# One transposed copy moved from ScalarE to VectorE, with other stage priorities, in a hybrid decoder layer

## The chip, the cores and the metric

One core of a Trainium2 chip runs the kernel. The metric is device microseconds of one execution. The kernel before takes 232.57 us, the median of 3 runs (232.31 to 232.76). Engines are named as the profile names them: PE is TensorE (PEld its weight loads), DVE is VectorE, ACT is ScalarE, POOL is GpSimd, SP is SyncE, which issues most DMAs.

## What is computed

One decoder layer on x (1 x 256 x 1024, float32). One projection of x is cut into four groups of 6 heads of 64 channels each; each group's output is gated, all four are concatenated, projected back to 1024 columns, and added to x under a layer norm:

```python
p = x @ w_in                                   # 1024 -> 5906 columns, four groups
y_a = moba_attention(...)  * silu(a_g)         # causal softmax attention, ALiBi
y_b = rms_norm(ssd_mixer(...) * silu(s_z))     # Mamba-2 scan, chunks of 128
y_c = dilated_attention(...) * silu(c_g)       # softmax over three dilations
y_d = rms_norm(gated_delta_chunked(...)) * silu(d_g)
out = layer_norm(alpha * x + concat(y_a, y_b, y_c, y_d) @ w_out)
```

The part that the change touches belongs to the gated delta rule. In chunks of 64 tokens it needs the inverse of a unit lower triangular matrix for each head:

```python
Lm = where(strict, (k * beta) @ k.T * decay, 0)
T = triangular_solve(eye + Lm, eye, lower=True, unit_diagonal=True)
u = T @ (v * beta)
w = T @ (k * beta * exp(g_cum))
```

## The kernel before

The float32 projections run as three matmul passes over high and low parts in float32r: `split` (line 447) takes a block of weights that `load` (432) brought by DMA into `raw`, copies it to `whi` on ScalarE, and VectorE subtracts to get `wlo`; TensorE then multiplies hi by hi, lo by hi, hi by lo. Rings of four `raw`, four `whi` and four `wlo` buffers keep this stream in program order. Around the stream stand the stages of the four groups: convolutions ("conv ..."), gates, decays, "norm k", "products" (which makes the matrices `M` and `A`), "blocks", "join", "delta", "state" and "scan", "scores", "values" and "attention" for the two softmax groups a and c, then "out" and the layer norms.

"blocks" starts at line 806. It inverts the 48 diagonal blocks of 32 x 32 (12 head-chunks of 128 tokens, 4 blocks each). Four DMAs move the blocks of `M` to DRAM (`dM`), one brings them back with one block on each of 48 partitions (`BL`, line 817). Then 31 elimination steps of two VectorE instructions each (a product into `tmp`, a subtraction into `Ub`) build the inverse, 62 instructions in sequence. `Tb`, the transposed copy of `Ub` inside each partition, is made at line 825; `Tb` goes to DRAM as `dT`, `Ub` as `dU`, and both come back as `T` (a part of the tile `TZ`) and `U`, spread over the 128 partitions. "join" combines pairs of 32-blocks to blocks of 64 with small matmuls, and "delta" (848) runs the recurrence. Memory is shared by tags: `BL` lies where the decay matrix `E` of the delta group was (tag s4), and `biasa`, the biases of attention a (977), come into the same place later.

The order on every engine isn't the program's. `Plan.run` (221) simulates a list schedule with costs written in the code and gives each engine its order; the order on an engine is then fixed, SP's DMAs included. Each operation has a rank: its `way` to the end, in us of the planner's costs, plus a bias, which is the stage's entry in `PRIO` and a correction for single steps in `STEPS`. `AHEAD` lets an engine wait a little for an operation of better rank, `LIMIT` says how many of the eight PSUM banks a kind of tile may hold at once, `STICK` favours matmuls of the mode that TensorE is in. The lines that decide:

```python
rank = [-int(o["way"] * 1000 + 0.5) - math.floor(o["bias"] * 1000 + 0.5) for o in ops]
...
t = min(at.values()) + AHEAD.get(e, 0.0)
k = min((max(at[i], t), rank[i] - stay(ops[i]), i) for i in at)
```

Every instruction is recorded through the planner, so nearly all have line 381 in the profile; tiles tell them apart.

Of the kernel before, what the change touches and what calls it, by code (L numbers as in the profile page):

```python
# [12 lines left out]
AF = mybir.ActivationFunctionType  # L13
# [37 lines left out]
def _biases():  # L51
# [12 lines left out]
NSM = 478  # L64
WARM = 8
STREAM = 1.0
SWITCH, PORT, AHEAD = 0.17, 0.9, {"dve": 0.033, "pe": 0.172, "pool": 0.066}
CUTS = (((0, 512), (512, 512)), ((0, 512), (512, 256), (768, 256)))
SHARE = [[slice(a, b) for a, b in v] for v in (
    ((0, 256), (256, 512)), ((512, 1024),), ((0, 512), (512, 1024)), ((0, 384), (384, 768), (768, 1024)))]  # L70
HELD = 5
HOLD = {10: (("hold_hi", "cvg", 1), ("hold_lo", "s3", 1))}
PRIO = {"split": -6.8, "conv k": 146.3, "gate d": -1265.8, "conv q": 1492.8, "gate s": 701.0, "steps": 1693.7,
        "decay d": 1542.9, "norm k": 4481.3, "products": 382.5, "norm q": 5697.9, "decay s": -3554.0,
        "values c": 663.3, "conv v": 174.6, "blocks": 42.6, "join": -2709.8, "delta": 4073.4, "conv bc": 149.8,
        "conv x": -58.8, "state": -630.8, "scan": 3483.0, "scores c": -913.9, "attention c": 9085.5,
        "scores a": 5133.5, "values a": -8452.1, "attention a": 1239.3, "out": -958.7, "out 0": -3694.0,
        "out 1": -5902.3, "ln 0": -1382.8, "ln 1": -1514.8}
CONST = -5, -4, -3
NRAW = 4  # L80
POOL = (6,)
POOLS = {"ps": (8, 512, F), "work": (3, W, F), "workd": (2, W, F), "workx": (1, W, F), "workg": (2, W, F), "cy": (3, S, F), "p": (3, W, F), "mx": (3, 4, F), "pt": (3, W, F), "oss": (2, 6, F), "sss": (2, 1, F), "srs": (2, 1, F)}
RINGS = {"raw": 4, "whi": 4, "wlo": 4}
STEPS = {"conv q 0": {"pe": -2.7}, "gate s 4": {"dve": -198.5}, "products 2": {"dve": 421.0},
# [9 lines left out]
         "attention a 5": {"dve": 0.6, "act": 142.2}, "attention a 6": {"act": -596.3},  # L94
         "attention a 10": {"act": -288.8}, "out 4": {"pe": 22.2}}
LIMIT = {"pj": 6, "g": 3, "ed": 6, "es": 6, "n": 4, "m": 5, "d": 2, "o": 4, "td": 2, "b": 1, "s": 2, "ts": 5, "c": 3, "ct": 6, "cv": 4, "a": 6, "at": 1, "av": 1}
BEGIN, SLOW = 1.2, 2.5
BESIDE = {(64, 128): 0.85, (128, 64): 0.62}
STICK = 1.0


class Plan:
# [289 lines left out]
def hybrid_layer(ctx, tc, plan, xT, x, w_in, w_out, convw, small, ln_g, ln_b, cst, biases, out):  # L392
    nc = tc.nc
    pe, act, dve, pool, sp = (plan.engine(n, e) for n, e in (
        ("pe", nc.tensor), ("act", nc.scalar), ("dve", nc.vector), ("pool", nc.gpsimd), ("sp", nc.sync)))
    pj = plan.engine("pe", nc.tensor, True)
# [94 lines left out]
    b = bank("pj")  # L491
# [244 lines left out]
    b = bank("ed")  # L736
# [7 lines left out]
    for i in range(2):  # L744
        b = bank("n")
# [12 lines left out]
        b = bank("n")  # L758
# [19 lines left out]
    for i in range(2):  # L778
        b, sq = bank("n"), work()
# [17 lines left out]
    for i in range(2):  # L797
        b = bank("n")
# [14 lines left out]
    BL, Ub, Tb = (t[:, :1024].rearrange("p (a b) -> p a b", a=32) for t in (BL, UbT, Tb))  # L813
# [6 lines left out]
    for j in range(31, 0, -1):  # L820
        n = 32 - j
        tv = tmp[:, :j * n].rearrange("p (a b) -> p a b", a=j)
        dve.tensor_mul(tv, BL[:, 0:j, j:j + 1].to_broadcast([48, j, n]), Ub[:, j:j + 1, j:32].to_broadcast([48, j, n]))
        dve.tensor_sub(Ub[:, 0:j, j:32], Ub[:, 0:j, j:32], tv)
    act.activation(Tb, Ub.rearrange("p a b -> p b a"), AF.Copy)
    sp.dma_start(dT, Tb)
    sp.dma_start(dU, Ub)
    for k in range(0, 4, 2):
# [274 lines left out]
```

## Time and profile before

| | us |
|---|---|
| median of 3 runs | 232.57 (232.31 to 232.76) |
| profiled execution | 233.04 |
| its span, first to last instruction | 231.3 |
| busy PE, DVE, ACT, POOL | 218.9, 174.5, 140.0, 24.2 |
| mean granted TensorE clock | 0.994 |

The span is shorter than the execution's own time by what lies around it. Busy shares are means over stages with different limits, so they have to be read by stretch; idle time counts only on the engine that holds up the end, and there the question is what ended it.

### The profile page before, as it was taken

To read this page: it belongs to the slowest core of one execution; us is meant where nothing else is said; L and a number is where in the kernel's file an instruction comes from. 1 tells how busy PE (TensorE), PEld (TensorE's weight loads), DVE (VectorE), ACT (ScalarE), POOL (GpSimd) and SP (SyncE) were. 2 spreads that over 40 slices of the span, in tenths; PEclk is the share of its full clock that TensorE was granted. 3 is DMA by queue.
4 is the path that set the end of the run, shared out by engine and by line. 5 is a ranking of instruction groups with operands and counts; after the bars stand their busy time and mean duration, and the time that the engine had idled before them with its cause. 6 is when DMAs were issued, how large, how long until landed. Compare 5 with 4: busy or idle time off the path is not lost. (4 is left out here: it accounts for less than half of the span.)

```text
span 231.3 us, 4530 instructions
## 1 busy us (share of the span) xinstructions
PE 218.9 (95%) x1679; PEld 202.6 (88%) x1679; DVE 174.5 (75%) x414; ACT 140.0 (61%) x297; POOL 24.2 (10%) x28
## 2 busy tenths in 40 slices
PE   8999999999999999999989999798999999999970
PEld 3999899998989999999979998687889998888870
DVE  2764999998599989998999984351677996635274
ACT  4765965738953666754469936999932854442210
POOL 7005021200110000000000000000221300000071
PEclk9999999999999999999999999999999999999997
DMA  5999766893934975489550249940523052663013
GB/s 170 312 335 361 209 195 201 211 241 81 273 102 102 234 187 155 128 225 277 150 163 29 68 101 320 270 110 9 180 67 119 1 184 91 211 242 94 0 68 113
DMA packets 46101, 38.10 MB, mean 165 GB/s; under 512 B 5616, under 2 KB 42608, under 8 KB 46080
## 3 DMA queue, kind: packets, MB, share of 16 engines
q1 hardware_dynamic: 45648, 37.43, 55.2%
q10 hardware_dynamic: 432, 0.39, 0.5%
q8 instruction: 13, 0.21, 0.4%
q14 instruction: 8, 0.07, 0.1%
HBM read 36.18 MB, written 1.64 MB: 163 GB/s over the span
## 5 line engine op out<-in xcount | busy, mean ns | idle before, releaser
L381 ACT ACTIVATE whi<-raw 128x1024 fp32r<-128x1024 f32 (+3 forms) x57 | 56.9, 1004 | 40.9 <-PE ps L381 31.1
L381 DVE TENSOR_TENSOR wlo<-raw,whi 128x1024 fp32r<-128x1024 f32 (+3 forms) x56 | 64.2, 1154 | 21.3 <-ACT whi L381 17.5
L381 PE MATMUL ps<-xhi,whi 128*128 128x256 f32 x272 | 41.9, 289 | 0.2
L381 PE MATMUL ps<-xlo,whi 128*128 128x256 f32 x272 | 41.8, 286 | 0.0
L381 PE MATMUL ps<-xhi,wlo 128*128 128x256 f32 x272 | 39.8, 284 | 0.0
L381 PEld LDWEIGHTS ps<-xhi,whi 128*128 128x128 f32 x272 | 36.0, 190 | 2.6 <-ACT whi L381 1.5
L381 PEld LDWEIGHTS ps<-xlo,whi 128*128 128x128 f32 x272 | 36.4, 191 | 0.8 <-issue 0.3
L381 PEld LDWEIGHTS ps<-xhi,wlo 128*128 128x128 f32 x272 | 35.7, 189 | 0.0
L381 PE MATMUL ps<-whi,mix 128*128 128x512 f32 (+1 forms) x110 | 28.7, 350 | 0.0
L381 ACT ACTIVATE p<-p,mx 128x256 f32<-128x256 f32 (+1 forms) x48 | 19.5, 444 | 3.6 <-DVE mx L381 3.6
L381 PEld LDWEIGHTS ps<-whi,mix 128*128 128x128 f32 x110 | 19.1, 188 | 2.7
L381 DVE SCALAR_TENSOR_TENSOR cy<-ps,cw,cy 128x253 f32<-128x253 f32 (+2 forms) x48 | 20.8, 473 | 0.8 <-ACT cy L381 0.7
L381 PE MATMUL ps<-wlo,mix 128*128 128x512 f32 (+1 forms) x55 | 19.3, 350 | 0.0
L381 PE MATMUL ps<-whi,xlo 128*128 128x384 f32 (+2 forms) x64 | 17.3, 344 | 0.0
L381 PE MATMUL ps<-whi,xhi 128*128 128x384 f32 (+2 forms) x64 | 16.9, 345 | 0.0
L381 PE MATMUL ps<-wlo,xhi 128*128 128x384 f32 (+2 forms) x64 | 16.4, 340 | 0.0
L381 POOL TENSOR_SCALAR_AFFINE_SELECT Es<-Es 128x1536 f32<-128x1536 f32 x1 | 1.5, 1548 | 100.7 <-ACT Es L381 100.7
L381 PEld LDWEIGHTS ps<-whi,xlo 128*128 128x128 f32 x64 | 11.6, 188 | 0.1
L381 PEld LDWEIGHTS ps<-wlo,xhi 128*128 128x128 f32 x64 | 11.6, 188 | 0.1
L381 PEld LDWEIGHTS ps<-whi,xhi 128*128 128x128 f32 x64 | 11.2, 188 | 0.5 <-ACT whi L381 0.2
L381 PEld LDWEIGHTS ps<-wlo,mix 128*128 128x128 f32 x55 | 10.4, 188 | 1.4
L381 DVE TENSOR_TENSOR Ub<-Ub 48x31 f32<-48x31 f32 (+15 forms) x31 | 10.3, 332 | 0.7
(219 smaller groups left out, 309.4 us busy)
## 6 DMA issues: line engine op xcount, KB each, us to landing
raw<-in_w_in_dram SPq DMA_DIRECT2D x30, 512.0 KB, 4.4
raw<-in_w_out_dram SPq DMA_DIRECT2D x12, 512.0 KB, 3.4
raw<-in_w_in_dram SPq DMA_DIRECT2D x8, 384.0 KB, 3.3
lead<-in_w_in_dram SPq DMA_DIRECT2D x7, 256.0 KB, 5.0
raw<-in_w_in_dram SPq DMA_DIRECT2D x4, 396.0 KB, 6.6
raw<-in_w_in_dram SPq DMA_DIRECT2D x4, 390.0 KB, 4.7
x<-in_x_dram SPq DMA_DIRECT2D x2, 512.0 KB, 5.1
xr<-in_xT_dram SPq DMA_DIRECT2D x7, 128.0 KB, 5.0
```

Of the source, the lines that this page charges most:

```text
L381: self.plan.add(eng, lambda: f(*a, **k), cost, outs, ins, dma, mode, port or (eng == "pool" and not dma), place, slow)
```

## The change

The copy of `Ub`, transposed inside each partition, into `Tb` is made by VectorE's `tensor_copy` instead of ScalarE's activation with the function Copy. The two DMAs behind it and everything else that is computed stay. The tables that the planner ranks by have other values: `PRIO` for each stage, `STEPS` for single steps, `LIMIT` for 12 of its kinds, `AHEAD` (no entry for GpSimd any more, VectorE's 0.038 in place of 0.033) and `STICK` (5.0 in place of 1.0). With them the order on every engine can differ.

```diff
@@ -64,39 +64,39 @@
 NSM = 478
 WARM = 8
 STREAM = 1.0
-SWITCH, PORT, AHEAD = 0.17, 0.9, {"dve": 0.033, "pe": 0.172, "pool": 0.066}
+SWITCH, PORT, AHEAD = 0.17, 0.9, {"dve": 0.038, "pe": 0.172}
 CUTS = (((0, 512), (512, 512)), ((0, 512), (512, 256), (768, 256)))
 SHARE = [[slice(a, b) for a, b in v] for v in (
     ((0, 256), (256, 512)), ((512, 1024),), ((0, 512), (512, 1024)), ((0, 384), (384, 768), (768, 1024)))]
 HELD = 5
 HOLD = {10: (("hold_hi", "cvg", 1), ("hold_lo", "s3", 1))}
-PRIO = {"split": -6.8, "conv k": 146.3, "gate d": -1265.8, "conv q": 1492.8, "gate s": 701.0, "steps": 1693.7,
-        "decay d": 1542.9, "norm k": 4481.3, "products": 382.5, "norm q": 5697.9, "decay s": -3554.0,
-        "values c": 663.3, "conv v": 174.6, "blocks": 42.6, "join": -2709.8, "delta": 4073.4, "conv bc": 149.8,
-        "conv x": -58.8, "state": -630.8, "scan": 3483.0, "scores c": -913.9, "attention c": 9085.5,
-        "scores a": 5133.5, "values a": -8452.1, "attention a": 1239.3, "out": -958.7, "out 0": -3694.0,
-        "out 1": -5902.3, "ln 0": -1382.8, "ln 1": -1514.8}
+PRIO = {"split": -6.8, "conv k": 261.5, "gate d": -1103.0, "conv q": 2491.5, "gate s": 854.7, "steps": 959.8,
+        "decay d": 1365.0, "norm k": 3635.6, "products": 309.8, "norm q": 6289.3, "decay s": -3915.3,
+        "values c": 756.8, "conv v": 164.5, "blocks": 659.4, "join": -2148.0, "delta": 5895.1, "conv bc": 151.7,
+        "conv x": -1545.1, "state": -1603.0, "scan": 1806.4, "scores c": -1852.9, "attention c": 8700.6,
+        "scores a": 5582.8, "values a": -6773.5, "attention a": 279.6, "out": -172.9, "out 0": -2742.4,
+        "out 1": -6301.6, "ln 0": -357.4, "ln 1": -2147.1}
 CONST = -5, -4, -3
 NRAW = 4
 POOL = (6,)
 POOLS = {"ps": (8, 512, F), "work": (3, W, F), "workd": (2, W, F), "workx": (1, W, F), "workg": (2, W, F), "cy": (3, S, F), "p": (3, W, F), "mx": (3, 4, F), "pt": (3, W, F), "oss": (2, 6, F), "sss": (2, 1, F), "srs": (2, 1, F)}
 RINGS = {"raw": 4, "whi": 4, "wlo": 4}
-STEPS = {"conv q 0": {"pe": -2.7}, "gate s 4": {"dve": -198.5}, "products 2": {"dve": 421.0},
-         "values c 1": {"pe": -170.4}, "values c 3": {"pe": -72.9}, "conv v 1": {"pe": 468.1},
-         "delta 6": {"pe": -9.9}, "conv bc 1": {"dve": -32.7}, "conv bc 2": {"dve": 93.5, "pe": -2.3},
-         "conv x 0": {"dve": 91.0}, "conv x 2": {"dve": -38.6},
-         "scores c q 2": {"dve": 44.6, "pe": 161.4}, "scores c k 1": {"pe": 58.2},
-         "scores c k 2": {"pe": 29.3}, "attention c 2": {"act": -39.3},
-         "attention c 5": {"act": -123.9}, "attention c 6": {"dve": 134.5, "pe": 56.8},
-         "attention c 9": {"pe": 44.5}, "attention c 10": {"dve": 4.9, "pe": 22.8},
-         "scores a k 2": {"pe": 64.6}, "values a 1": {"pe": 460.5}, "attention a 0": {"pe": -0.2},
-         "attention a 1": {"act": 12.1}, "attention a 2": {"act": 1.5}, "attention a 4": {"pe": -0.1},
-         "attention a 5": {"dve": 0.6, "act": 142.2}, "attention a 6": {"act": -596.3},
-         "attention a 10": {"act": -288.8}, "out 4": {"pe": 22.2}}
-LIMIT = {"pj": 6, "g": 3, "ed": 6, "es": 6, "n": 4, "m": 5, "d": 2, "o": 4, "td": 2, "b": 1, "s": 2, "ts": 5, "c": 3, "ct": 6, "cv": 4, "a": 6, "at": 1, "av": 1}
+STEPS = {"conv q 0": {"pe": -36.8}, "gate s 4": {"dve": -212.7}, "products 2": {"dve": 290.2},
+         "products 4": {"dve": -58.6}, "values c 0": {"pe": 26.5}, "values c 1": {"pe": -203.2},
+         "values c 2": {"pe": 26.6}, "conv v 0": {"pe": 332.1}, "conv v 1": {"dve": -76.4},
+         "delta 2": {"pe": 4.2}, "conv bc 0": {"act": 102.4, "dve": 75.4}, "conv bc 2": {"pe": -3.4},
+         "conv x 0": {"pe": 1.9}, "conv x 1": {"dve": -117.8, "pe": 5.6}, "conv x 2": {"dve": -16.3},
+         "state": {"pe": 107.2}, "scores c k 0": {"pe": -422.2}, "attention c 1": {"act": 32.7},
+         "attention c 2": {"dve": -44.4}, "attention c 5": {"pe": -2.2},
+         "attention c 6": {"act": 179.6}, "attention c 7": {"pe": -93.8},
+         "attention c 9": {"dve": -47.1, "act": 156.4}, "attention c 10": {"act": 82.1},
+         "values a 1": {"pe": 127.3}, "attention a 0": {"pe": -0.2}, "attention a 1": {"act": 70.0},
+         "attention a 2": {"act": 12.6}, "attention a 5": {"act": 414.1},
+         "attention a 6": {"act": -44.5}, "attention a 10": {"act": -4.1}, "out 4": {"pe": 62.0}}
+LIMIT = {"pj": 6, "g": 2, "ed": 6, "es": 3, "n": 6, "m": 4, "d": 5, "o": 3, "td": 3, "b": 1, "s": 4, "ts": 3, "c": 6, "ct": 4, "cv": 5, "a": 6, "at": 1, "av": 1}
 BEGIN, SLOW = 1.2, 2.5
 BESIDE = {(64, 128): 0.85, (128, 64): 0.62}
-STICK = 1.0
+STICK = 5.0
 
 
 class Plan:
@@ -822,7 +822,7 @@
         tv = tmp[:, :j * n].rearrange("p (a b) -> p a b", a=j)
         dve.tensor_mul(tv, BL[:, 0:j, j:j + 1].to_broadcast([48, j, n]), Ub[:, j:j + 1, j:32].to_broadcast([48, j, n]))
         dve.tensor_sub(Ub[:, 0:j, j:32], Ub[:, 0:j, j:32], tv)
-    act.activation(Tb, Ub.rearrange("p a b -> p b a"), AF.Copy)
+    dve.tensor_copy(Tb, Ub.rearrange("p a b -> p b a"))
     sp.dma_start(dT, Tb)
     sp.dma_start(dU, Ub)
     for k in range(0, 4, 2):
```

## Rows read from the trace of the kernel before

**Rows 1.** The page, part 1: busy us, share of the span, instructions
```profile
PE 218.9 (95%) x1679; PEld 202.6 (88%) x1679; DVE 174.5 (75%) x414; ACT 140.0 (61%) x297; POOL 24.2 (10%) x28
```

**Rows 2.** Chain that ended last: start us, us, what (its longest piece)
```profile
167.37 56.85 PE ps L381 x378
```

**Rows 3.** Two windows: PE, PEld, DVE, ACT, POOL busy (instructions), clock, DMA share, GB/s
```profile
70.00:140.00 70.00, 68.90 (x572) 67.42 (x571) 66.57 (x172) 44.13 (x94) 0.00 (x0) 1.00 0.59 155
...
140.00:170.00 30.00, 27.49 (x304) 23.98 (x303) 13.96 (x46) 26.06 (x72) 1.55 (x1) 1.00 0.53 161
```

**Rows 4.** Timeline: start us, us, engine, operation, tiles; idle before and its releaser
```profile
121.69 0.55 PE L381 MATMUL ps<-csb,p 128*128 128x128 f32 x3 [1.10 <-ACT p L381]
...
154.40 0.83 PEld L381 LDWEIGHTS ps<-TZ,M 32*32 32x32 f32 x48 [0.25 <-issue]
...
155.73 0.55 PE L381 MATMUL ps<-csb,p 128*128 128x128 f32 x3 [0.39 <-ACT p L381]
...
160.16 0.91 PE L381 MATMUL ps<-vb,U 64*64 64x64 f32 x12 [0.54 <-ACT U L381]
...
162.12 0.91 PE L381 MATMUL ps<-u,M 64*64 64x64 f32 x12 [0.27 <-ACT u L381]
```

**Rows 5.** Timeline around the copy and behind it, 138 to 148 us
```profile
138.24 0.34 SPq L381 DMA_DIRECT2D biasa<-in_biases_dram  x1
138.25 0.18 DVE L381 TENSOR_TENSOR Ub<-Ub 48x31 f32<-48x31 f32 x1
...
139.10 2.13 ACT L381 ACTIVATE Tb<-Ub 48x1024 f32<-48x1024 f32 x1
139.35 0.96 DVE L381 TENSOR_TENSOR wlo<-raw,whi 128x768 fp32r<-128x768 f32 x1 [0.92 <-PE ps L381]
...
140.75 1.02 PEld L381 LDWEIGHTS ps<-xhi,wlo 128*128 128x128 f32 x8
...
141.25 0.32 SPq L381 DMA_DIRECT2D dT<-Tb  x1
...
141.67 0.39 SPq L381 DMA_DIRECT2D raw<-in_w_in_dram  x1
...
144.05 0.42 DVE L381 CUSTOM_DVE_ANT_0 p<-ps,biasa 128x256 f32<-128x256 f32 x1 [0.83 <-DMA biasa<-in_biases_dram]
...
144.52 0.51 ACT L381 ACTIVATE p<-p,mx 128x256 f32<-128x256 f32 x1 [2.02 <-DVE mx L381]
...
147.13 0.55 PE L381 MATMUL ps<-csb,p 128*128 128x128 f32 x3 [1.24 <-ACT p L381]
```

**Rows 6.** Groups by form: engine, operation, tiles, shapes, count; busy us, mean ns; idle
```profile
L381 DVE TENSOR_TENSOR wlo<-raw,whi 128x1024 fp32r<-128x1024 f32 x41 | 50.0, 1224 | 15.2 <-ACT whi L381 12.3 <-PE ps L381 2.4
...
L381 DVE TENSOR_SCALAR sp<-sp 128x24 f32<-128x24 f32 x2 | 0.3, 175 | 0.0
...
L381 DVE TENSOR_SCALAR cw<-cw 128x80 f32<-128x80 f32 x1 | 0.2, 192 | 0.0
...
L381 ACT ACTIVATE whi<-raw 128x1024 fp32r<-128x1024 f32 x41 | 43.4, 1063 | 33.8 <-PE ps L381 27.3 <-DMA raw<-in_w_out_dram 5.4 <-DMA raw<-in_w_in_dram 0.9
```

**Rows 7.** Tiles M and BL: count, duration ns min/median/max, first and last start us
```profile
L381 DVE SCALAR_TENSOR_TENSOR M<-ps,rk,Ed x12: 334/334/339, 65.5 to 72.4; 128x128 f32<-128x128 f32 x12
L381 SPq DMA_DIRECT2D dM<-M x4: 327/454/707, 72.7 to 84.8; - x4
...
L381 DVE TENSOR_TENSOR Ub<-BL,Ub x31: 182/349/417, 98.9 to 138.0; 48x31 f32<-48x31 f32 x2, 48x60 f32<-48x60 f32 x2, 48x87 f32<-48x87 f32 x2, 48x112 f32<-48x112 f32 x2
L381 SPq DMA_DIRECT2D BL<-dM x1: 451/451/451, 92.4 to 92.4; - x1
```

**Rows 8.** DMA issues: tiles, queue, count, KB each, median us from issue to landing
```profile
dM<-M SPq DMA_DIRECT2D x4, 48.0 KB, 4.0
BL<-dM SPq DMA_DIRECT2D x1, 192.0 KB, 4.7
```

**Rows 9.** Window of the elimination, instructions on Ub: DVE, ACT, POOL busy, clock, DMA
```profile
98.80:138.50 39.70, 20.54 (x62) 0.00 (x0) 0.00 (x0) 1.00 0.53 145
```

## The prediction

> **What bounds the kernel now.** I began with the busy shares of the page. TensorE is busy for 218.9 of 231.3 us, VectorE for 174.5 and ScalarE for 140.0 [rows 1]: whatever the change does to VectorE and ScalarE, it can show in the time only through moments in which TensorE has nothing to do. The chain of work that ended last says where such moments can still matter: from 167.37 us on it is one unbroken piece of TensorE, 56.85 us long, ending at 224.2 us, with the layer norm behind it [rows 2]. So nothing is to be had after 167 us unless work is moved there or away from there; the amount of matmul work isn't touched by the change. Next I cut the time before it into two stretches. From 70 to 140 us TensorE is busy 68.90 of 70 and VectorE 66.57 of 70, while ScalarE has 44.13. From 140 to 170 us it is the other way round: TensorE 27.49 of 30, VectorE 13.96, ScalarE 26.06 [rows 3]. [...] The reader is to see two things. TensorE's idle time is small: 1.10 us in the first stretch, 2.51 us in the second, 3.61 us in sum. And VectorE is nearly full up to 140 us and half empty behind it, with ScalarE the fuller one there.
>
> Last, the timeline at TensorE's idle places. There are five that matter from 118 us on: 1.10 us at 121.69 (attention c's first softmax), 1.24 us at 147.13 (attention a's first softmax), and 0.39, 0.54 and 0.27 us at 155.73, 160.16 and 162.12. ScalarE ended every one of them [rows 4, 5].
>
> **The copy itself.** The transposed copy runs now on ScalarE from 139.10 to 141.23, 2.13 us. It becomes one VectorE instruction behind the last subtraction into `Ub`, which starts at 138.25 and ends at 138.43 [rows 5]. Its duration on VectorE isn't in the trace: no VectorE row reads with a stride. Nearest above: VectorE's own pass over 1024 contiguous elements takes 1.224 us [rows 6], and ScalarE's strided 2.127 us against its contiguous 1.063 us [rows 6, 5] is a factor of 2.0, which would make 2.45 us. Nearest below: VectorE's one-input operations take 0.175 us at 24 elements and 0.192 us at 80 [rows 6], 0.0003 us an element, which would make 0.48 us. I take 1.22 us, since that row has the same number of elements.
>
> [...] ScalarE's strided row is twice its contiguous one. [...]
>
> What waits behind the copy on VectorE: the `wlo` subtraction that now starts at 139.35, after 0.92 us in which VectorE is idle. With a copy of 1.22 us from 138.43 to 139.65 it starts 0.30 us later and ends at 140.61 instead of 140.31; TensorE loads it as weights from 140.75 on [rows 5]. So in the present order the copy is hidden up to 0.92 + 0.44 = 1.36 us, and costs nothing; at 2.45 us it would cost TensorE 1.1 us. Cost taken: 0, bounds 0 and 1.1.
>
> What it frees: `dT` leaves at 141.25 now and could leave at about 139.7, 1.5 us earlier, and the DMA of weights behind it in SP's queue, at 141.67, moves up likewise [rows 5]. But nothing at TensorE waits for `T`: TensorE's load of the join's first weights, at 154.40, follows a pause of 0.25 us that its own issue ended, not a transfer [rows 4]. So the shorter chain gives TensorE nothing by itself. ScalarE is rid of 2.13 us just ahead of the stretch in which it is 87% busy; that I count below.
>
> **The new order.** `PRIO` is added to an operation's way to the end, in us, and its differences (hundreds) are larger than any way (below 232), so it ranks the stages; the ranks count only among operations that could start at nearly the same time. Most stages keep their place or nearly. The one that moves far is "blocks", 42.6 to 659.4: from behind "products", "attention a", "conv k", "conv v" and "conv bc" to ahead of all five. "delta" passes "scores a" as well. In the trace, the last operation on `M` starts at 72.4 us, yet the four transfers `dM` go out between 72.7 and 84.8, with DMAs of weights between them in SP's queue, and `BL` at 92.4, landing 4.7 us later; the elimination starts at 98.9 [rows 7, 8]. Issued back to back, the four (some 0.45 us each) and their 4.0 us to landing, then 4.7 us for `BL` [rows 8], would let it start near 84 to 86 us, 13 to 15 us earlier. Its 62 instructions need 20.54 us of VectorE wherever they stand; they took 39.7 us because other work lies between them [rows 9]. So I expect its end some 8 to 15 us earlier, near 123 to 130 us. SP's DMAs of weights then stand behind four small transfers, about 1.8 us once; they are issued several us ahead of their use, so I take 0 (bounds 0 and one stall of the kind seen, 1.24).
>
> What an earlier end of the elimination gives TensorE:
> First, the biases of attention a. `biasa` lies in the memory of `BL`, so its load is issued at 138.24, just behind the elimination's last reading of `BL` at 138.0 [rows 7], and VectorE waits 0.83 us for it at 144.05; ScalarE's softmax follows, and TensorE's 1.24 us at 147.13 behind that [rows 5]. The load would come early: gain taken 0.83, bounds 0 and 1.24.
> Second, join and delta can start earlier, away from the stretch where ScalarE evacuates for softmax, decays and delta at once, and ScalarE has 2.13 us less in front of it. The three stalls there are 0.39 + 0.54 + 0.27 = 1.20 us [rows 4]. They are one-step-after-another work and some of it stays wherever it stands; I take half, 0.60, bounds 0 and 1.20.
> Third, the stall of 1.10 at 121.69 is a softmax's own latency; gain 0, bounds 0 and 1.10.
> Against it, an order that differs everywhere (the limits on PSUM banks for 12 kinds, `STICK` 1 to 5, single steps) has stalls of its own that no row shows. The stalls seen run from 0.27 to 1.24 us; I charge the smallest, 0.27, bounds minus 0.27 and 1.24.
>
> Sum on the profiled execution: its span of 231.30 less 0.83 and 0.60 plus 0.27, so 230.14. Around the span lie 1.74 us (it took 233.04), which gives 231.88; it lay 0.47 above the median of 232.57. Against the median: 232.57 - 1.16 = 231.41. A measurement of this kernel can tell about 0.2%, 0.47 us, from no change.
>
> **The rivals.**
> *VectorE becomes the bound.* Place: 84 to 140 us. VectorE has 3.43 us free from 70 to 140 [rows 3]. The elimination now comes first there, so the `wlo` subtractions (1.224 us each) that feed TensorE's projections stand behind it, and the copy comes on top, in this full stretch instead of the empty one, since the elimination ends before 130. From the point at which the free 3.43 us are used up or lie at the wrong moment, each us of VectorE is a us of TensorE. Price: the copy, 1.22, up to 2.45. Time 233.8 (up to 235.0). For it: 95% busy. Against it: `wlo` operations stand between the elimination's steps now too, and an elimination that starts early leaves VectorE emptier at 125 to 140. [...] Chance 0.27.
> *It is hidden anyway.* TensorE's idle time moves to other places with the same sum: whatever is pulled forward stalls there for the same latencies. Time 232.5. For it: only 3.61 us are idle in 100 us. Chance 0.17. The case that the elimination isn't earlier after all belongs here.
> *All of it goes.* The stalls at 147.13, 155.73, 160.16, 162.12 and 121.69 all vanish: 1.24 + 1.20 + 1.10 = 3.54 us, 229.0. For it: ScalarE ends them all. Against: softmax and delta are serial. Chance 0.06.
>
> **How the numbers follow.** The forecast, 231.4 with chance 0.50, has a range of its own from 230.1 (both gains whole) to 232.1. Faster is that and the last rival, 0.56; same 0.17; slower 0.27. The range of 8 in 10 goes down to 229.8, which leaves out most of the last rival (0.05), and up to 234.0, which holds the middle of the slower one and leaves out its upper part (0.12).
>
> **What would show it.** Right: `BL` is issued before 86 us, the last `Ub` before 131; the copy takes about 1.2 us on VectorE; `biasa` lands before attention a's first VectorE operation and the stall there is under 0.5; TensorE's idle time from 140 to 170 us falls from 2.51 to near 1.3, and that of 70 to 140 stays near 1.1. Wrong: idle time from 80 to 140 us above 2 us, with VectorE's `wlo` as its end; or a copy above 2 us inside the full stretch; or the unbroken piece of TensorE at the end getting longer, because work was pushed behind 170 us.

## The result, and the profile after

The changed kernel takes 233.75 us, the median of 17 runs (232.67 to 235.69), beside 232.73 us for the kernel before, in 17 runs of its own. Four of before's runs (235.74 to 239.14 us) lie more than 1.5% above its fastest and stay out of the ratio, which is 1.0080, 95% interval [1.0055, 1.0105]; with them in, the means of the two sets of 17 would differ by 0.8 us. By the ratio the changed kernel is slower, by 1.9 us. I had forecast 231.4, 1.2 us faster; the time lies in the range (229.8 to 234.0), on the side that I gave 0.27. The profiled execution took 233.84 us with a span of 232.1.

The page, part 1, as in [rows 1]:

```profile
PE 218.6 (94%) x1679; PEld 201.5 (87%) x1679; DVE 174.9 (75%) x415; ACT 137.5 (59%) x296; POOL 24.0 (10%) x28
```

The chain that ended last, its longest piece, as in [rows 2], and the two windows of [rows 3] (PE, PEld, DVE, ACT, POOL busy, clock, DMA share, GB/s):

```profile
168.26 56.78 PE ps L381 x378
```

```profile
70.00:140.00 70.00, 68.90 (x571) 67.37 (x571) 67.69 (x173) 43.02 (x94) 0.00 (x0) 1.00 0.60 153
140.00:170.00 30.00, 26.92 (x296) 23.27 (x294) 13.42 (x44) 24.79 (x70) 1.55 (x1) 1.00 0.53 164
```

The unbroken piece of TensorE is as long as before and starts 0.89 us later. TensorE's idle time between 140 and 170 us has grown from 2.51 to 3.08 us, where I had expected 1.3; VectorE has 1.12 us more to do up to 140 us, about the copy.

The elimination, by its tiles (count, ns min/median/max, first and last start), as in [rows 7], and SP's timeline ahead of it:

```profile
L381 DVE TENSOR_TENSOR Ub<-BL,Ub x31: 182/350/417, 100.8 to 138.3; 48x31 f32<-48x31 f32 x2, 48x60 f32<-48x60 f32 x2, 48x87 f32<-48x87 f32 x2, 48x112 f32<-48x112 f32 x2
L381 SPq DMA_DIRECT2D BL<-dM x1: 447/447/447, 93.7 to 93.7; - x1
```

```profile
72.36 0.34 SPq L381 DMA_DIRECT2D dM<-M  x1
74.00 2.64 SPq L381 DMA_DIRECT2D raw<-in_w_in_dram  x3
76.69 1.75 SPq L381 DMA_DIRECT2D dM<-M  x1
80.34 3.00 SPq L381 DMA_DIRECT2D raw<-in_w_in_dram  x2
83.39 0.58 SPq L381 DMA_DIRECT2D dM<-M  x1
86.38 2.11 SPq L381 DMA_DIRECT2D raw<-in_w_in_dram  x2
88.54 0.59 SPq L381 DMA_DIRECT2D dM<-M  x1
93.17 0.37 SPq L381 DMA_DIRECT2D raw<-in_w_in_dram  x1
93.72 0.45 SPq L381 DMA_DIRECT2D BL<-dM  x1
```

None of this is earlier, but for the first `dM`. The four `dM` still have weight loads between them, the fourth leaves 3.7 us later than before, `BL` 1.3 us later, the first `Ub` starts at 100.8 in place of 98.9, the last product at 138.3 in place of 138.0.

The timeline around the copy and at TensorE's pauses behind it, as in [rows 4] and [rows 5]:

```profile
138.53 0.34 SPq L381 DMA_DIRECT2D biasa<-in_biases_dram  x1
138.75 1.13 DVE L381 COPY Tb<-Ub 48x1024 f32<-48x1024 f32 x1
...
139.91 0.32 SPq L381 DMA_DIRECT2D dT<-Tb  x1
...
144.80 0.42 DVE L381 CUSTOM_DVE_ANT_0 p<-ps,biasa 128x256 f32<-128x256 f32 x1 [1.48 <-DMA biasa<-in_biases_dram]
...
145.50 0.61 PE L381 MATMUL ps<-whi,xhi 128*128 128x384 f32 x2 [0.65 <-DVE mx L381]
...
148.37 0.55 PE L381 MATMUL ps<-csb,p 128*128 128x128 f32 x3 [1.22 <-ACT p L381]
...
156.48 0.55 PE L381 MATMUL ps<-csb,p 128*128 128x128 f32 x3 [0.20 <-ACT p L381]
...
158.29 0.95 PE L381 MATMUL ps<-U,TZ 32*32 32x32 f32 x48 [0.21 <-ACT TZ L381]
...
160.54 0.91 PE L381 MATMUL ps<-vb,U 64*64 64x64 f32 x12 [0.40 <-ACT U L381]
...
162.75 0.91 PE L381 MATMUL ps<-u,M 64*64 64x64 f32 x12 [0.28 <-ACT u L381]
```

The copy is what the change says: 1.13 us on VectorE, 2.13 on ScalarE before, and `dT` leaves 1.34 us earlier. But `biasa` still leaves behind the last `Ub`, VectorE waits 1.48 us for it in place of 0.83, and TensorE pauses twice behind that, 0.65 us and 1.22 us, where it paused once before, 1.24 us.

### The profile page after: what moved, and what is told of

Read it like the earlier page. It is cut to its first block, busy times and chain, and to the rows that moved or that the text cites. A ratio compares the mean times of both kernels' runs of the same rounds, so it can differ in the third digit from the quotient of the medians.

```text
span 232.1 us, 4530 instructions
## 1 busy us (share of the span) xinstructions
PE 218.6 (94%) x1679; PEld 201.5 (87%) x1679; DVE 174.9 (75%) x415; ACT 137.5 (59%) x296; POOL 24.0 (10%) x28
## 5 line engine op out<-in xcount | busy, mean ns | idle before, releaser
L381 PE MATMUL ps<-xlo,whi 128*128 128x256 f32 x272 | 42.5, 284 | 0.0
L381 PE MATMUL ps<-xhi,wlo 128*128 128x256 f32 x272 | 40.7, 283 | 0.0
L381 ACT ACTIVATE cy<-ps,cw 128x256 f32<-128x256 f32 x16 | 8.8, 563 | 4.8 <-PE ps L381 2.5
```

The source lines that it names most:

```text
L381: self.plan.add(eng, lambda: f(*a, **k), cost, outs, ins, dma, mode, port or (eng == "pool" and not dma), place, slow)
```

## The experiments

Each ratio is to the kernel before, run on the same chip, with its 95% interval.

**The copy or the tables.** Two kernels with half of the change each, and the changed kernel once more.

```diff
 # copy_alone: the tables of before, and
-    act.activation(Tb, Ub.rearrange("p a b -> p b a"), AF.Copy)
+    dve.tensor_copy(Tb, Ub.rearrange("p a b -> p b a"))
 # tables_alone: the tables of the change, and the copy as it was
```

> The copy alone moves to VectorE, all tables as before; the order on every engine stays as it was but for the copy itself. Theory A (the lost time comes from the new order): within 0.3 us of the kernel before, since the copy's 1.13 us lies in VectorE's idle 0.92 us ahead of the wlo subtraction and 0.44 us of cover behind that; dT leaves near 139.7, 1.5 us earlier; the stalls of TensorE near 147 and 155 to 162 stay. Rival B (the copy costs): 1.0 to 1.9 us slower, the wlo subtraction behind the copy ends late and TensorE has a new pause near 141. Rival C (the measured slowdown is a drift between runs): no difference here and none in the next two.

> The tables of the change with the copy still on ScalarE. Theory A: 1.0 to 1.9 us slower than before, as slow as the whole change. Rival B: within 0.3 us of before. Rival C: no difference.

> The whole change, on the same chip as the two halves. Theory A and rival B: 1.0 to 1.9 us slower than before. Rival C: within 0.4 us of before.

Measured: the copy alone 1.0024 [1.0000, 1.0047], and 1.0025 [0.9991, 1.0060] when it was run again; the tables alone 1.0089 [1.0053, 1.0124]; the changed kernel again 1.0089 [1.0050, 1.0127]. So the loss is in the order that the tables make; which of the five tables makes it was not taken apart. The copy gains nothing, and costs between nothing and 1.1 us by the first interval.

**Which stretch of the order.** Four kernels with the copy on VectorE whose order is that of one set of tables up to a planned time and that of the other behind it.

```diff
+def _until(order):
+    return sum(1 for i in order if _until.at[i] < 72.0)
+
+def _splice(one, two, until):
+    n = until(one)
+    head = one[:n]
+    done = set(head)
+    return head + [i for i in two if i not in done]
 # late_two: before's order up to 72, the changed one behind; first_only: the reverse
 # tail_only: before's order up to 112 (116 us in the trace), the changed one behind; no_tail: the reverse
```

> Order of the kernel before up to the end of the products (about 72 us), order of the change from there on; the copy on VectorE in this and the next three. Theory D (the stretch from 72 to 118 us costs: VectorE's convolutions go ahead of wlo, the weight buffers come free late, the weights land late, VectorE reaches attention c's first softmax late and TensorE's quiet stretch there grows until the clock falls): 1.0 to 1.9 us slower than before, softmax c later than 119.2, ScalarE waits about 3 us for a weight DMA near 97. Rival E (the swaps behind 142 us cost): 0.5 to 1.0 slower, no such wait. Rival F (the order up to 72 us costs): within 0.4 of before.

> Order of the change up to about 72 us, order of before from there on. D and E: within 0.5 us of before. F: 1.0 to 1.9 us slower.

> Order of before up to attention c's first softmax (about 116 us), order of the change behind it. [...] E: 0.5 to 1.9 us slower.

> Order of the change up to about 116 us, order of before behind it. D: 1.0 to 1.9 us slower, clock low near 122 us in part of the executions. E: within 0.4 us of before. F: 1.0 to 1.9 us slower.

Measured: late_two 1.0040 [0.9999, 1.0082], first_only 1.0101 [1.0050, 1.0153], tail_only 1.0000 [0.9966, 1.0035], no_tail 1.0066 [1.0032, 1.0100]. The new order behind 116 us shows no cost, within 0.8 us, as D and F would have it; ahead of it it costs about as much as the whole change, and the part up to 72 us is enough for that. So nothing speaks for E, the swaps behind 142 us (its smallest cost, 0.5 us, is still inside the interval of tail_only). first_only has the number of F, the order up to 72 us, which D had at nothing, and late_two a part of that of D, the stretch behind it.

To see where the time goes I compared the starts of like matmuls (same tiles, shape and count) with those in the execution of before, as medians in us over some 8 us from the time in the heading; a minus is earlier than before. first_only has before's order from 72 us on, no_tail from 116 us on, and tail_only up to 116 us:

| execution | at 24 | at 72 | at 114 | at 132 | at 174 |
|---|---|---|---|---|---|
| copy alone | -0.17 | -0.48 | -0.49 | -0.49 | -0.69 |
| tail_only | -0.03 | -0.33 | -0.33 | -0.33 | 0.39 |
| no_tail | -0.88 | -0.14 | -0.13 | -0.12 | 0.74 |
| first_only | -0.57 | -0.25 | -0.26 | 2.06 | 2.04 |
| changed | -0.57 | 0.10 | 0.10 | 0.29 | 0.80 |
| changed, again | -1.15 | -0.25 | -0.27 | 1.75 | 1.75 |
| tables alone | -0.34 | 0.12 | 0.12 | 2.68 | 2.27 |

Between 24 and 72 us the new order loses 0.3 to 0.9 us in these executions, where before's order gains 0.3 (in later ones before's order gains up to 0.3 or loses up to 0.4, and the new one loses between 0.0 and 1.0, where nothing was changed in it by hand up to 72 us). But it loses there what it had gained up to 24 us: at 72 us it is within 0.3 us of the execution of before, and up to 0.6 us behind the two others with before's order. Like executions differ by as much at 72 us (before's order lies between -1.0 and 0.5 in later ones), so a net cost up to there isn't clear of the scatter. Nothing happens from 72 to 114 us. Then, between 114 and 132 us, the executions with the new order ahead of that lose nothing, 0.2, or 2.0 to 2.6 us; among the last is first_only, which runs before's order at that time. From 132 to 174 us changed, tail_only and no_tail lose 0.5 to 0.9 us more, and this too in either order.

**What happens at 118 us.** Here TensorE runs the 24 score matmuls of attention c and then waits for its softmax [rows 4]. First before, then the changed kernel's second execution; start, us, engine, operation, tiles:

```profile
117.85 2.74 PE L381 MATMUL ps<-cqk 64*128 64x128 f32 x24
...
118.99 0.41 DVE L381 CUSTOM_DVE_ANT_0 p<-ps,biasc 128x256 f32<-128x256 f32 x1
```

```profile
117.59 3.26 PE L381 MATMUL ps<-cqk 64*128 64x128 f32 x24
...
119.24 0.41 DVE L381 CUSTOM_DVE_ANT_0 p<-ps,biasc 128x256 f32<-128x256 f32 x1
...
121.95 0.73 PE L381 MATMUL ps<-csb,p 128*128 128x128 f32 x3 [1.10 <-ACT p L381]
```

From first score to first softmax operation it was 1.14 us before and 1.65 us here; from first score to first transposition 3.84 and 4.36. VectorE came later, and TensorE's stretch grew by as much. The same in other executions, with VectorE's waits for `whi` between 74 and 122 us beside it (last column: the granted clock behind the stretch, 0.50 where it fell to that level):

| execution | VectorE waited for whi | score to softmax | score to transposition | clock behind |
|---|---|---|---|---|
| before; copy alone | 0.4; 0.4 | 1.14; 1.15 | 3.84; 3.85 | 1.00 |
| no_tail; tail_only | 0.2; 0.7 | 1.14; 1.14 | 3.85; 3.84 | 1.00 |
| changed | 0.8 | 1.33 | 4.03 | 1.00 |
| changed, again | 1.2 | 1.65 | 4.36 | 0.50 |
| first_only | 1.4 | 1.94 | 4.65 | 0.50 |
| tables alone | 1.7 | 2.21 | 4.91 | 0.50 |
| fill_pause | 2.0 | 2.49 | 5.20 | 1.00 |
| wlo_on_pool | 0.5 | 2.86 | 5.56 | 0.50 |

In every line the third number is 2.70 or 2.71 us above the second: what VectorE is late beyond 1.14 us, TensorE pays one for one. The two executions of the changed kernel and fill_pause have the same order up to there and lie 0.2, 0.5 and 1.4 us above 1.14: how late VectorE is differs from execution to execution. On top of it the granted clock fell in some executions. Windows of the changed kernel's second execution, from the first score on:

```profile
117.59:122.17 4.58, 3.37 (x27) 2.49 (x27) 4.55 (x20) 2.53 (x11) 0.00 (x0) 1.00 0.77 202
122.17:125.58 3.41, 3.41 (x16) 3.22 (x15) 3.22 (x14) 3.41 (x15) 0.00 (x0) 0.50 0.01 3
```

For 3.41 us the clock is 0.50, after 4.58 us in which TensorE was busy for 3.37 with small matmuls. Such a fall costs 1.5 us: the execution lost 2.02 us between 114 and 132 us, 0.52 of it by the longer stretch; the tables alone lost 2.56, 1.07 of it by the stretch.

**Filling the pause.** So the first suspect was the clock.

```diff
+                for _ in range(9):
+                    nc.tensor.matmul(banks[-1][:, 384:512], xhi[:, 0, 0:128], xhi[:, 0, 0:128], start=True, stop=True)
                 # ahead of the first transposition of p in attention c
```

> The changed kernel in its own order, with nine matmuls of 128 columns added that nobody reads: TensorE runs them behind the last scores of attention c, where it otherwise pauses 1.10 us for ScalarE's first p (row at 121.98 of the changed kernel). They do work that isn't needed, and leave nothing out. Theory G (a part of the loss is TensorE's clock, which falls to half for 3.41 us behind the quiet stretch of scores and pause wherever that stretch lasts 4.36 us or more): no stretch at half clock near 122 us in any execution, mean granted clock 0.989 or more in all undisturbed ones, and the median 0.4 to 0.8 us under the changed kernel's, a ratio to the kernel before of 1.003 to 1.006. Theory H (the clock falls by chance and not by that stretch, and the whole loss is stalls of the order): executions at a mean clock of 0.982 to 0.984 stay, a ratio of 1.007 to 1.010.

Measured: 1.0113 [1.0074, 1.0152], from 6 runs, all with a mean clock of 0.992 or more. No run has the low mean clock, as theory G says, and the time didn't come back, as theory H says. In its profile the clock stays at 1.00 and the nine matmuls end just ahead of the transposition, but VectorE had come later than in any run so far (2.49 us, table), ahead of the matmuls that were added. So the loss is there without the fall of the clock, which comes on top in single executions.

**Softmax first, weights first.** Two kernels in which I moved VectorE's operations by hand.

```diff
 # softmax_first: VectorE's operations that stand just ahead go behind the first halves of two softmaxes
+    late = [i for i in plan.found[0] if plan.ops[i]["eng"] == "dve" and at[soft[0]] - 2.0 <= at[i] < at[soft[0]]]
+    for n, i in enumerate(late):
+        at[i] = at[soft[3]] + 0.001 * (n + 1)
 # weights_first: the halves of the weights go 3 us ahead
+    for o in plan.marks["weights"]:
+        if 58.0 <= at[o] < 112.0:
+            at[o] -= 3.0
```

> The changed kernel, its order left as it is but for four operations of VectorE: the first halves of the first two softmaxes of attention c go ahead of a wlo and an Ub that stand before them (the wlo took 1.21 us at 117.81 in the changed kernel). Theory G with VectorE as its cause: the stretch from the first score to the first transposition of p, 4.03 to 4.36 us in the changed kernel, gets 0.5 to 1.0 us shorter, no half clock behind it, ratio 1.003 to 1.006. If the stretch isn't made by VectorE's lateness, it stays at 4.0 us or more, with executions at 0.982 to 0.984, and the ratio at 1.007 to 1.010.

> The changed kernel with whi and wlo, the two halves of each weight block, about 3 us earlier among the other operations of ScalarE and VectorE from 58 to 112 us; TensorE's and the loads' orders are those of the changed kernel. Theory K (the loss is made by the loop of four raw buffers: wlo frees one, the next load is issued, lands 3.7 to 5.8 us later, and whi waits for it; in the new order this loop has no slack, so VectorE comes to attention c late): ScalarE's waits for raw between 74 and 122 us fall from 6.0 to 10.9 us in all to under 4 us, the first softmax of attention c starts under 118.8 us, ratio to the kernel before 1.001 to 1.005. The rival (VectorE is late since it has too much to do in that stretch, whatever stands first): the waits for raw fall, but the softmax stays at 119.2 us or later and the ratio at 1.007 to 1.012, with TensorE waiting for the convolutions that now stand behind.

Measured: 1.0186 [1.0143, 1.0229] and 1.0563 [1.0515, 1.0612]. Neither tells the theories apart. In the first the `wlo` came to stand between the halves of the softmaxes, so PSUM's banks came free later and the last scores waited 1.23 us for VectorE. Its stretch of scores and pause was 5.66 us, and the clock stayed at 1.00 behind it: a long stretch doesn't always bring the fall. In the second VectorE stood 5.33 us at 64.76 in front of a `wlo` that couldn't run yet. An order that is moved in one place by hand makes waits in others.

**A fifth buffer.** Between 74 and 122 us ScalarE waits three times for a weight load in the changed kernel's execution, and once in that of before (us in all, times, longest; before first):

```profile
ACT whi L381 <- DMA raw<-in_w_in_dram: 0.4, 1, 0.4
```

```profile
ACT whi L381 <- DMA raw<-in_w_in_dram: 6.0, 3, 3.0
```

```diff
-        raw = blocks(new("raw", 1024), k, n)
+        late = plan.stage in FIFTH
+        turn[0] += late
+        spare = late and turn[0] % 5 == 1 and (plan.force is not None or plan.found)
+        raw = blocks(new("raw", 1024, tag="aqk" if spare else None), k, n)
```

> The changed kernel with the orders of TensorE, ScalarE and VectorE untouched, but every fifth weight load from conv q to scores c goes into the buffer of aqk, which is unused then: the loop of raw buffers has five places in place of four, so a load can be issued one wlo earlier. Theory K (weight loads without slack make VectorE late for attention c): ScalarE's waits for raw between 74 and 122 us fall from 6.0 to 10.9 us in all to under 3 us, VectorE's idle time at 98 and 113 us goes, TensorE doesn't wait at 114 to 120 us for VectorE beyond what before has, executions at a clock of 0.982 to 0.984 get rare, and the median is 0.5 to 1.2 us under the changed kernel's: ratio 1.002 to 1.006. What is left over 1 is what the order costs up to 72 us (0.5 to 0.8 us by the shift of like matmuls). The rival (the loads only share the queues with each other, so that earlier loads land no earlier; or VectorE is late by its amount of work): waits or the softmax of attention c stay as they are, ratio 1.007 to 1.011.

> The same with biasa issued three loads earlier as well and BL in Tb's buffer: both causes taken away from the changed kernel, its orders kept. If the two are separate: 1.0 to 1.3 us under the fifth buffer alone, ratio to the kernel before 0.996 to 1.001. If one hides the other: like after_biasa, 1.001 to 1.005.

Measured: 1.0103 [1.0057, 1.0150], and 1.0060 [1.0035, 1.0084] with `biasa` early as well. The changed kernel's three waits end at 78.0, 90.9 and 97.9 us. With the fifth buffer in use, from 74 to 96 us, the last two are gone and 4.0 us of waiting are left in all, not the under 3 us that theory K asks for; VectorE waits 2.4 us for `whi` and still comes 1.78 us behind the first score. From 100 us on only four buffers were in use, and the loads left at 103.66, 105.45 and 107.73 as in the changed kernel at 103.68, 105.47 and 107.74. So this doesn't decide on K, though two of the waits that it blames went without a gain. What `biasa` is worth shows again, 0.43%.

**Work taken off VectorE.**

```diff
-            (pool if count in POOL else dve).tensor_sub(lo[:, r, c], src[:, r, c], f32(hi[:, r, c]))
+            (pool if count in POOL or len(plan.ops) in SPARE else dve).tensor_sub(lo[:, r, c], src[:, r, c], f32(hi[:, r, c]))
```

> The changed kernel with the orders kept and two of VectorE's wlo between 88 and 104 us (1.21 us each) given to GpSimd, which does nothing from 64 to 165 us. VectorE so has 2.4 us less to do ahead of attention c. Theory L (VectorE has no slack up to attention c, and what it is late there TensorE waits for): the first softmax comes within 1.2 us of the first score in place of 1.33 to 2.21, TensorE's stretch of scores and pause is 3.85 us or less in place of 4.03 to 4.91, no half clock near 122 us, and the median is 0.4 to 1.0 us under the changed kernel's: ratio 1.002 to 1.006. The rival (what is late is the weights themselves, or GpSimd's longer wlo holds up VectorE or the next loads): VectorE's waits for whi grow by what it was relieved of, stretch and ratio stay, 1.007 to 1.011.

Measured: 1.0201 [1.0140, 1.0261]. Timeline of the two moved subtractions and of what stood still beside them on VectorE:

```profile
87.29 2.84 POOL L389 TENSOR_TENSOR wlo<-raw,whi 128x1024 fp32r<-128x1024 f32 x1 [21.88 <-ACT cy L389]
...
88.30 2.13 DVE L389 SCALAR_TENSOR_TENSOR bcT<-bcT,cy 128x256 f32<-128x256 f32 x1
...
100.82 2.67 POOL L389 TENSOR_TENSOR wlo<-raw,whi 128x1024 fp32r<-128x1024 f32 x1 [10.69 <-ACT whi L389]
...
101.53 2.00 DVE L389 TENSOR_TENSOR Ub<-BL,Ub 48x31 f32<-48x31 f32 x1
```

An `Ub` operation of 0.18 us [rows 7] takes 2.00 us and ends with GpSimd's, at 103.5 us; a convolution's last step, 0.41 us elsewhere, takes 2.13 us and ends 0.3 us behind GpSimd's. VectorE wasn't relieved but stopped, came 2.86 us behind the first score, and TensorE's stretch was 5.56 us: the one-for-one rule of the table, by the other way in. That VectorE's lateness is what TensorE pays is so shown; that the changed kernel can be made fast by more room on VectorE isn't.

**biasa by itself.** The first term of my sum, made without the new order: the copy alone, with `biasa` issued three loads earlier and `BL` in other memory.

```diff
-    ... ("BL", 1024, "s4"), ...
+    ... ("BL", 1024, "s4" if plan.force is None and not plan.found else "mix3"), ...
 # in SP's order:
+    at[plan.marks["biasa"]] -= 14
```

> The tables of before and the copy on VectorE, each engine's order as in that experiment, with one difference: the blocks' BL lies in the buffer of Tb, so that biasa doesn't have to wait for the last Ub, and biasa is issued three weight loads earlier, near 122 us in place of 137.8. This takes the first term of my sum alone. The forecast's step (0.83 us of wait for biasa are on the path): VectorE's wait of 0.82 us at 143.37 is gone, TensorE's pause of 1.24 us behind it falls to 0.3 to 0.6 us, and the time is 0.6 to 0.9 us under that of the copy alone: ratio to the kernel before 0.997 to 0.9995. The rival (what is gained there is waited for further on, at the join of the blocks or for u): the wait is gone, but the pauses between 150 and 165 us grow by as much, ratio 1.000 to 1.004 as with the copy alone.

> The tables of before and the copy on VectorE once more, on the chip of the next run, as its reference: ratio to the kernel before 0.999 to 1.004.

> The copy on VectorE with biasa issued early, once more, beside the copy alone on one chip: 0.8 to 1.1 us under the copy alone, ratio to the kernel before 0.996 to 0.999, if the wait for biasa is what the first term of my sum says; within 0.3 us of the copy alone if the earlier difference was chance.

> The changed kernel in its own order, with biasa issued three weight loads earlier and BL in the buffer of Tb, as in the experiment on the copy alone. If the wait for biasa is the same kind of loss in the changed kernel: its 1.48 us of VectorE's wait at 144.80 is gone, and the median is 0.8 to 1.2 us under the changed kernel's, ratio to the kernel before 1.003 to 1.005. If the changed kernel's loss ahead of it hides the wait: ratio 1.007 to 1.011 as without.

Measured: 0.9979 [0.9961, 0.9996]; again, beside the copy alone on one chip, 0.9960 [0.9926, 0.9994] against 1.0025 [0.9991, 1.0060]; in the changed kernel 1.0022 [0.9990, 1.0055], where that has 1.0080. The same edit gives 0.45 to 0.65%, 1.0 to 1.5 us (the first pair and the last are compared across chips). On the copy alone it is a little faster than the kernel before, by 0.2 and 0.4%. Timeline of the first (SP, VectorE, TensorE's pauses):

```profile
118.66 0.57 SPq L388 DMA_DIRECT2D biasa<-in_biases_dram  x1
...
142.42 0.42 DVE L388 CUSTOM_DVE_ANT_0 p<-ps,biasa 128x256 f32<-128x256 f32 x1
...
145.49 0.55 PE L388 MATMUL ps<-csb,p 128*128 128x128 f32 x3 [0.36 <-ACT p L388]
...
154.09 0.55 PE L388 MATMUL ps<-csb,p 128*128 128x128 f32 x3 [0.39 <-ACT p L388]
...
158.52 0.91 PE L388 MATMUL ps<-vb,U 64*64 64x64 f32 x12 [0.54 <-ACT U L388]
...
160.48 0.91 PE L388 MATMUL ps<-u,M 64*64 64x64 f32 x12 [0.27 <-ACT u L388]
```

No wait for `biasa`; the pause of 1.24 us is 0.36. The three behind it are those of [rows 4] to a hundredth.

**The elimination made early.** What I took the priorities to do, done by hand: `dM` and `BL` on ScalarE's queue as soon as `M` is there, the `Ub` operations and what follows them 14 us earlier in their engines' orders.

```diff
-        sp.dma_start(dM[12 * k:12 * k + 12].rearrange("h p c -> p h c"), M[r, :, r])
-    sp.dma_start(BL, dM)
+        act.dma_start(dM[12 * k:12 * k + 12].rearrange("h p c -> p h c"), M[r, :, r])
+    act.dma_start(BL, dM)
 # in the order:
+    gain = 14.0
+    for i in ids[7:] + [plan.marks["biasa"]]:
+        at[i] -= gain
```

> The tables of before and the copy on VectorE, with the elimination really made early: dM and BL are issued on ScalarE's queue as soon as M is made, 73 to 78 us, and the Ub operations, the copy, dU, dT and biasa stand about 14 us earlier in their engines' orders than before; all else keeps its order. This is what the forecast took the new priorities to do. The forecast: first Ub near 84 us, last near 124, no wait for biasa, TensorE idle 1.2 to 1.6 us in place of 2.5 between 140 and 170 us, and under 0.3 us more between 70 and 140: ratio to the kernel before 0.994 to 0.998. The rival, VectorE becomes the bound: wlo comes late behind the Ub operations, TensorE waits over 1 us for wlo or for scores between 84 and 125 us, ratio 1.004 to 1.012.

Measured: 1.0441 [1.0394, 1.0488], 10 us slower. The transfers on ScalarE's queue, the products into `Ub`, and TensorE's pauses:

```profile
71.72 2.79 ACTq L388 DMA_DIRECT2D dM<-M  x4
...
78.14 0.32 ACTq L388 DMA_DIRECT2D BL<-dM  x1
```

```profile
L388 DVE TENSOR_TENSOR Ub<-BL,Ub x31: 182/349/417, 87.1 to 132.2; 48x31 f32<-48x31 f32 x2, 48x60 f32<-48x60 f32 x2, 48x87 f32<-48x87 f32 x2, 48x112 f32<-48x112 f32 x2
```

```profile
99.09 1.42 PE L388 MATMUL ps<-bcT 128*128 128x128 f32 x6 [2.73 <-DVE bcT L388]
...
127.27 1.65 PE L388 MATMUL ps<-cqk 64*128 64x128 f32 x4 [3.63 <-DVE mx L388]
...
155.72 0.55 PE L388 MATMUL ps<-csb,p 128*128 128x128 f32 x3 [0.36 <-ACT p L388]
...
164.32 0.55 PE L388 MATMUL ps<-csb,p 128*128 128x128 f32 x3 [0.39 <-ACT p L388]
...
168.75 0.91 PE L388 MATMUL ps<-vb,U 64*64 64x64 f32 x12 [0.54 <-ACT U L388]
...
170.71 0.91 PE L388 MATMUL ps<-u,M 64*64 64x64 f32 x12 [0.26 <-ACT u L388]
```

The elimination starts 12 us earlier and ends only 6 us earlier, since VectorE has no room for it; TensorE waits 2.73 us for the convolutions and 3.63 us for attention c. A part of the 10 us is the clock, which fell in this execution; window, busy us and granted clock as in [rows 3]:

```profile
116.00:134.00 18.00, 13.53 (x91) 12.02 (x90) 16.55 (x55) 10.60 (x31) 0.00 (x0) 0.81 0.47 119
```

The clock's means, 0.98, 0.91 and 0.81 in the windows from 84 to 100, to 116 and to 134 us, are those of some 10 us at 0.50 and the rest at 1.00: three times the 3.41 us that cost 1.5 us at 118 us, an estimate of 4.5 us. Behind it the wait for `biasa` is gone, and the other three pauses are again the same, though the elimination ended earlier; join and delta had kept their places in the engines' orders.

## Why the prediction was wrong

**The step that failed** is "The new order": from "blocks" at 659.4 I concluded that the four `dM` and `BL` would go out back to back, the elimination start near 84 to 86 us, and `biasa` come early. `BL` went out at 93.7. I had written in the same paragraph that ranks count only among operations that could start at nearly the same time, and didn't ask when the plan lets each `dM` start. By the plan's costs it can start 3.4 us after the end of the one before: `region` (154) takes the first dimension of the view `"h p c -> p h c"` for 32 rows of `dM`, the four views begin 12 rows apart, so each write seems to touch the one before, and `lat` (215) adds 0.9 + `SLOW`. The times that the changed kernel's own plan computes show it: the second to fourth `dM` and `BL` become free at 74.34, 80.74, 86.33 and 91.99 us and start at just these times. In the plan of the kernel before they become free at 74.76, 79.58, 85.62 and 90.29, and only two of them start later, by 0.26 and 0.48 us. So there was next to nothing that a better rank could take away. That the wait is the plan's, and nothing that the transfers need, shows in elim_early, where the four go out within 2.79 us.

Both gains, 0.83 and 0.60, hung on that step, and so did the first rival's place. The sign that I named, `BL` before 86 us, says so at once. The case had its sentence under "hidden anyway", but with 0.17 and no loss. And "blocks" wasn't the only stage that moved far: "attention a" went from 1239.3 to 279.6 and "conv x" from -58.8 to -1545.1, so I had looked at one move of many.

**The first term** was right as a price and too small. Taking the wait for `biasa` away gives 1.0 to 1.5 us on the copy alone, on the changed kernel and on the one with the fifth buffer, where I had 0.83, bounds 0 and 1.24. The 0.83 was VectorE's wait; TensorE's pause behind it fell by 0.88. In the changed kernel the wait didn't go, it grew to 1.48.

**The second term**, 0.60 for half of the three stalls in join and delta, didn't come: in the changed kernel the pauses there are 0.20, 0.21, 0.40 and 0.28 us, 1.09 in place of 1.20. Where the elimination ended 6 us earlier and ScalarE was rid of the copy they were 0.39, 0.54 and 0.26, as before. But join and delta stood where they had stood, so what an earlier place would give them isn't shown.

**The copy** was sized well (1.13 for 1.22). Its trace with the old tables shows it hidden: TensorE is 0.49 us ahead of before at 132 us and 0.69 ahead at 174. The ratios, 1.0024 and 1.0025, leave room for a small cost. The doubled time, 2.45, didn't come.

**The order's own stalls** were mis-sized: 0.27 us charged (bounds minus 0.27 and 1.24). The changed kernel's profiled execution is 0.80 us longer than before's, and by the table of shifts that is a gain of 0.57 up to 24 us, a loss of 0.67 up to 72, of 0.19 at 118 us, where VectorE comes late, and of 0.51 between 132 and 174, where the wait for `biasa` has grown. In other executions VectorE's lateness at 118 us costs up to 1.1 us, with 1.5 more where the clock falls there; the second execution and the tables alone show that fall. The wait for `biasa` is 1.70 and 1.88 us in tail_only and no_tail, in either order, and TensorE then has a pause of 0.86 and 0.83 us ahead of the one for the softmax. What each place makes of the 1.9 us over all runs isn't shown. Two numbers bound it. Six of the changed kernel's 17 runs had a mean clock of 0.982 to 0.987 and a median of 235.2 us; the other eleven, 0.989 or more, 233.4, which is still 1.1 us above the 232.3 of before's runs in the ratio. And an early `biasa` alone brings the changed kernel from 1.0080 to 1.0022, though it gains as much on the old tables.

**The rival "VectorE becomes the bound"** had the right engine and side and the wrong mechanism: nothing of the elimination moved. What a move does is seen in elim_early, where it was made by hand: 10 us slower, not 1.2. The 3.43 us that VectorE has free from 70 to 140 us [rows 3] can't take 20.54 us moved 14 us forward.

**What stays open.** Why VectorE comes late to attention c in the new order. Its waits for `whi` go with it in the table from 0.8 us on (wlo_on_pool, at 0.5, has another cause), but ScalarE's waits for weight loads don't: no_tail has 6.2 us of them, the changed kernel 6.0, and in no_tail VectorE isn't late. The fifth buffer didn't reach the last stretch ahead of attention c, and the other two edits brought waits of their own. first_only shows that the new order up to 72 us is enough for it; which of its moves isn't shown, nor why the clock falls behind some long stretches (4.36 us) and not behind others (5.66 us).

## What to carry to other kernels

A rank in a list schedule can't start an operation before the plan has it free: before costing what a priority moves, look up in the plan when each step of the chain becomes free and what it waits for, and whether that wait is real. Where an engine is 95% busy, as VectorE here, a serial chain placed earlier on it ended 6 us earlier for 12 and delayed the rest; taking the transfer that waited for the chain off it, by giving it other memory, gained 1.0 to 1.5 us in every kernel tried. An order tuned as a whole is best judged by the shift of like matmuls against the old trace, in several executions of each, since like executions differ by as much as a stretch may lose.

## What the hardware showed that I had not expected

The strided copy took 2.13 us on ScalarE, twice its contiguous pass of 1.063 us [rows 5, 6], and 1.09 to 1.14 us on VectorE in 17 executions, less than VectorE's contiguous pass of 1.224 us over as many elements with two inputs. What the stride costs on VectorE isn't shown: no run has its contiguous copy, and 1.13 us is over twice the 0.48 us that I estimated from its small one-input operations, 0.175 us at 24 elements and 0.192 us at 80 [rows 6].

Beside each of the two subtractions on GpSimd one operation of VectorE took far longer: 2.00 us in place of 0.18 for `Ub` above, and 2.13 in place of 0.41 for a convolution's last step, to the end of GpSimd's 2.67 us and 0.3 us beyond that of its 2.84 us. Other operations of VectorE kept their time beside the same two: `vb` took 0.55 us at 87.79, as at 92.63 where GpSimd was idle, and a convolution's step 0.48 us at 101.14. What makes the difference isn't shown.

TensorE's granted clock fell to 0.50 in some executions behind the stretch of small matmuls, for 3.41 us in the changed kernel's second, where the stretch took 4.36 us; in its first, of the same order, it stayed at 1.00 behind 4.03 us. In the six runs whose pause was filled the mean clock was 0.992 or more.
